# Moving a broadcast and the pool weights in the first loads, and carrying the PSUM turn from one phase to the next

## The chip, the cores and the metric

The kernel runs on the 8 NeuronCores of one Trainium2 chip (two dies, cores 0 to 3 and 4 to 7). Each core does one prompt sequence of 2048 tokens and 16 of the 128 sample tokens; no core waits for another. The metric is the device time of the slowest core in microseconds (us). Engines are called as the profile calls them: PE (matmuls), PEld (weight loads of PE), ACT, DVE, POOL, and SP, which here only issues DMAs. POOL issues DMAs too; those of the weight matrices here also turn f32 into bf16 (W_k, 1024 x 1024 values, lands as 2048 KB).

Some executions were in a slower state: one die then had a granted PE clock of 0.84 to 0.92 instead of 0.99, and the time was 1783 to 1920 us. Only fast executions are compared here.

## The reference, cut to what matters

Two layers. Layer 0 mixes tokens with causal pooling, layer 1 with a short gated convolution; after the mixer each layer has a cross-attention to 256 memory rows and a squared-ReLU MLP.

```
for i in range(2):
    u = rmsnorm(x, g_mix[i])
    if i == 0: y, st = pool_mixer(u, ...)   # window means minus the token, per-group 256x256 map w_pool, times scale
    else:      y, st = conv_mixer(u, ...)   # [B, C, h] = u @ W_in;  y = W_out(B * conv3(C * h))
    x = x + y
    x = x + mem_attend(rmsnorm(x, g_attn[i]), mem_k[i], mem_v[i], w_q[i], w_o[i])
    x = x + sq_relu_mlp(rmsnorm(x, g_ffn[i]), w_up[i], w_down[i])
return rmsnorm(x, g_final), ...             # also the last 15 normalised rows (times g_mix) of the pooling layer
```

## The kernel before: the parts that matter

Every operation is put on an engine's queue by a helper; the helpers find from the addresses who must wait for whom. An engine, and SP with its DMAs, works through its queue in order: a DMA that must wait holds up all later DMAs of its queue. In the kernel before (core 4), SP issued the g_mix broadcast only at 54.91 us, when the spill issued at 46.84 us had landed, and the next x load behind it at 55.39 us.

The **prelude** (about the first 100 us) loads the 16 blocks of x (128 tokens, 512 KB each), normalises them (stA), pools them (stB), transposes them and adds the mapped pooling (stC). Between these steps it prepares the memory rows. x goes through a ring of 7 buffers, so block `tb + 7` is loaded when stC has read block `tb`.

```
# GBC (the broadcast g_mix row) and MEMN1 (memory rows for layer 1) share their bytes
GBC = so.alloc(F32, [D]);  MEMN1 = T(GBC.off, BF16, [NCH, NMEM])
...
xload(0); dma(SP, GV2, gv); xload(1)
dma(POOL, SCB(), <pool_scale row, broadcast to 128 partitions>, "wpf")
dma(POOL, BANDS(), bands)
for cc in range(2):
    dma(POOL, WPF[cc](), wpool_d[:, cc*128:(cc+1)*128, :].rearrange("g p e -> p g e"), "wpf")   # runs of 1 KB
xload(2); <mem rows>; xload(3) .. xload(6)                      # SP
dma(POOL, SK(), W_k);  dma(POOL, SQ_(), W_q)
...
def poolw():                                    # the "scaling": WP = w_pool * g_mix * scale, eight DVE operations
    ...
def stC(tb):
    ...                                         # transposes, WP products, evacuation
    if tb + NXB < 16: xload(tb + NXB)
def mem_turn(k):                                # steps 3 and 4
    ...
    if k == 3:
        spill.append(dma(SP, memn_d, MEMN1))                    # write the memory rows to DRAM
        dma(SP, GBC(), <g_mix row, broadcast to 128 partitions>)  # must wait until the spill has landed
```

In its main loop step s runs stB(s-1), stC(s-2), stA(s+1), then extra work: gains in step 0, poolw in step 1, memory rows in steps 2 to 4, products with W_k from step 9 on.

**PSUM banks** are handed out in turn. Prelude and conv use eight banks, attention and MLP seven, because bank 7 holds the sums of the samples there. A matmul into a bank waits until whoever reads that bank has finished; at the start of layer 1's attention PE waited 3.56 us for such a read by DVE (core 4).

```
def nxt():
    b = bank_ctr[0] % bank_mod[0]; bank_ctr[0] += 1
    return b
def attn_phase(l, fill=()):
    bank_mod[0] = 7
    ...
```

The last conv tile ends with channel chunk 7, whose gate product (DVE) reads a bank at the very end. Right after it layer 1's attention starts: score product m=0, score product m=1, then the output product of that last conv tile (conv_out), which needs all gates.

The softmax here doesn't subtract the row's maximum and nothing guards it: scores larger than these inputs give would overflow.

## Time and profile before

| | before |
|---|---|
| time, median of 3 runs | 1661.63 us (1660.75 to 1663.36) |
| span of the profiled execution, slowest core (core 4) | 1663.1 us |
| PE busy | 1582.0 us, 95% |
| granted clock, mean of each core | 0.989 to 0.991 |

From the page of the kernel before: the span, the busy time of each engine, and the shares of the chain of work that ended last.

```profile
span 1663.1 us, 28460 instructions; the slowest of 8 cores (1656.8 to 1663.1 us)
...
PE 1582.0 (95%) x10064; PEld 902.0 (54%) x10064; DVE 876.0 (53%) x1934; ACT 567.0 (34%) x1074; POOL 114.6 (7%) x245
...
PE 88%; DVE 4%; DMA 2%; ACT 2%; issue 2%; DVEq 0%; POOL 0%; ACTq 0%; SPq 0%; POOLq 0%
```

PE, busy for 95% of the span and 88% of this chain, is the limit nearly everywhere, so the question is where it stands still. The same chain in order of time, in the prelude (start us, length us, what):

```profile
3.55 17.21 DMA MEM<-w_pool
20.86 0.28 DVE MEM L326
...
21.27 5.84 DVE MEM L326 x4
...
46.84 8.00 DMA memn<-MEM
...
54.91 0.33 SPq L353
...
55.39 14.11 DMA MEM<-x
```

First, everything hangs on w_pool's arrival and its scaling on DVE (L326). Then, at 46.84 us, on the spill (memn), on SP's issue of the g_mix broadcast behind it, and on an x load issued at 55.39 us that takes 14.11 us to land. The timeline of PE shows what it does meanwhile (start us, length us, engine, line, operation, count; in brackets the idle time before, and what ended it):

```profile
core 4 of [0, 1, 2, 3, 4, 5, 6, 7], span 1663.1 us
...
62.11 1.89 PE L291 MATMUL PS<-MEM 128*128 128x512 bf16 x8
72.50 4.71 PE L295 MATMUL PS<-MEM 128*128 128x128 bf16 x40 [8.50 <-ACT MEM L342]
77.01 2.44 PE L291 MATMUL PS<-MEM 128*128 128x512 bf16 x8
79.29 2.62 PE L295 MATMUL PS<-MEM 128*128 128x128 bf16 x40
```

PE stands for 8.50 us, and the first 40 matmuls after that take 4.71 us, where the same 40 take 2.62 us later. PE's other standstill of interest is at the start of layer 1's attention, in the timeline of PE:

```profile
core 4 of [0, 1, 2, 3, 4, 5, 6, 7], span 1663.1 us
...
985.93 4.27 PE L291 MATMUL PS<-MEM 128*128 128x400 bf16 x24 [1.01 <-DVE MEM L330]
993.75 6.52 PE L291 MATMUL PS<-MEM 128*128 128x416 bf16 x20 [3.56 <-DVE MEM L330]
```

### The profile page before, as it was taken

To read this page: it belongs to the slowest core of one execution; us is meant where nothing else is said; L and a number is where in the kernel's file an instruction comes from. 1 tells how busy PE (TensorE), PEld (TensorE's weight loads), DVE (VectorE), ACT (ScalarE), POOL (GpSimd) and SP (SyncE) were. 2 spreads that over 40 slices of the span, in tenths; PEclk is the share of its full clock that TensorE was granted. 3 is DMA by queue.
4 is the path that set the end of the run, shared out by engine and by line. 5 is a ranking of instruction groups with operands and counts; after the bars stand their busy time and mean duration, and the time that the engine had idled before them with its cause. 6 is when DMAs were issued, how large, how long until landed. Compare 5 with 4: busy or idle time off the path is not lost.

```text
span 1663.1 us, 28460 instructions; the slowest of 8 cores (1656.8 to 1663.1 us)
## 1 busy us (share of the span) xinstructions
PE 1582.0 (95%) x10064; PEld 902.0 (54%) x10064; DVE 876.0 (53%) x1934; ACT 567.0 (34%) x1074; POOL 114.6 (7%) x245
## 2 busy tenths in 40 slices
PE   3799999999999999999999989999999999999885
PEld 3675555555555555555555545555555655555543
DVE  4465675655444344436566665765564444432356
ACT  4566344541122222231222225444532111123542
POOL 2002110110000000000000001210110000000000
PEclk9899999999999999999999999999999999999998
DMA  9849794575537606246000027894546642000122
GB/s 234 200 78 155 159 168 99 117 147 79 87 67 126 112 1 102 30 76 104 1 1 1 1 44 123 161 174 110 115 90 102 100 61 57 1 1 1 42 80 85
DMA packets 84614, 145.14 MB, mean 87 GB/s; under 512 B 4334, under 2 KB 37358, under 8 KB 84460
## 3 DMA queue, kind: packets, MB, share of 16 engines
q0 software_dynamic: 67568, 84.08, 34.5%
q1 hardware_dynamic: 16908, 59.24, 10.5%
q8 instruction: 84, 1.38, 0.3%
q14 instruction: 54, 0.44, 0.1%
HBM read 212.42 MB, written 14.36 MB: 136 GB/s over the span
## 4 chain that ended last, share of the span: by engine, by line
PE 88%; DVE 4%; DMA 2%; ACT 2%; issue 2%; DVEq 0%; POOL 0%; ACTq 0%; SPq 0%; POOLq 0%
PE PS L291 86%; DVE MEM L326 2%; ACT MEM L318 2%; PE PS L295 2%; DVE MEM L347 1%; DMA MEM<-w_pool 1%; DMA MEM<-x 1%; DMA memn<-MEM 0%; ACT MEM L307 0%; PE PS L300 0%; DVE MEM L344 0%; DVE MEM L330 0%; DVE MEM L338 0%; ACT MEM L342 0%; POOL MEM L353 0%
## 5 line engine op out<-in xcount | busy, mean ns | idle before, releaser
L291 PE MATMUL PS<-MEM 128*128 128x416 bf16 (+5 forms) x8960 | 1503.1, 328 | 16.6 <-DVE MEM L326 7.3
L291 PEld LDWEIGHTS PS<-MEM 128*128 128x128 bf16 (+1 forms) x8960 | 832.3, 98 | 677.6 <-issue 56.0
L318 ACT ACTIVATE MEM<-PS 128x416 f32<-128x416 f32 (+6 forms) x509 | 260.3, 516 | 647.0 <-PE PS L291 626.1
L330 DVE TENSOR_TENSOR MEM<-PS,MEM 128x416 f32<-128x416 f32 (+5 forms) x525 | 294.9, 581 | 253.6 <-PE PS L291 245.3
L330 DVE TENSOR_TENSOR MEM<-MEM 128x416 bf16<-128x416 f32 (+3 forms) x282 | 160.0, 584 | 198.3 <-ACT MEM L318 189.8
L326 DVE SCALAR_TENSOR_TENSOR MEM<-MEM 128x416 bf16<-128x416 f32 (+7 forms) x322 | 181.1, 614 | 128.7 <-ACT MEM L318 107.7
L318 ACT ACTIVATE MEM<-MEM 128x416 bf16<-128x416 f32 (+10 forms) x305 | 186.2, 622 | 180.8 <-DVE MEM L330 113.3
L303 DVE SCALAR_TENSOR_TENSOR MEM<-MEM,PS 128x256 f32<-128x256 f32 x256 | 105.2, 420 | 72.4 <-PE PS L291 48.7
L295 PE MATMUL PS<-MEM 128*128 128x128 bf16 (+4 forms) x896 | 61.7, 248 | 31.2 <-DVE MEM L326 10.4
L342 ACT COPY MEM<-PS 128x512 f32<-128x512 f32 (+3 forms) x73 | 39.1, 536 | 130.3 <-PE PS L291 116.4
L295 PEld LDWEIGHTS PS<-MEM 128*128 128x128 bf16 (+2 forms) x896 | 48.8, 107 | 46.3 <-issue 44.8
L342 ACT CAST MEM<-PS 128x512 bf16<-128x512 f32 (+2 forms) x73 | 39.7, 555 | 66.2 <-PE PS L291 64.8
L344 DVE CAST MEM<-PS 128x512 bf16<-128x512 f32 (+1 forms) x68 | 43.8, 656 | 11.6 <-PE PS L291 11.6
L353 POOL DMA_DIRECT2D MEM<-cv x64 | 47.6, 744 | 13.8 <-PE PS L291 13.8
L318 ACT ACTIVATE PS<-PS 128x416 f32<-128x416 f32 (+3 forms) x67 | 33.1, 494 | 41.3 <-PE PS L291 41.1
L347 DVE TENSOR_REDUCE MEM<-MEM 128x1 f32<-128x1024 f32 (+2 forms) x20 | 24.2, 1209 | 40.8 <-ACT MEM L318 40.8
L300 PE MATMUL PS<-MEM 128*128 128x128 f32 (+6 forms) x208 | 25.1, 268 | 20.6 <-DVE MEM L326 9.8
L350 POOL MEMSET MEM<- 128x4 bf16 (+1 forms) x96 | 15.0, 159 | 358.9 <-PE PS L295 271.6
L326 DVE SCALAR_TENSOR_TENSOR MEM<-PS,MEM 128x512 f32<-128x512 f32 (+2 forms) x40 | 28.1, 743 | 15.5 <-ACT MEM L318 15.5
L300 PEld LDWEIGHTS PS<-MEM 128*128 128x128 f32 (+6 forms) x208 | 21.2, 133 | 24.3 <-issue 23.1
L338 DVE TENSOR_SCALAR MEM<-MEM 128x1024 bf16<-128x1024 f32 (+1 forms) x18 | 13.6, 753 | 36.9 <-ACT MEM L318 36.9
L353 POOL DMA_DIRECT2D MEM<-w_up x36 | 20.6, 582 | 138.0 <-PE PS L291 138.0
(27 smaller groups left out, 131.3 us busy)
## 6 DMA issues: line engine op xcount, KB each, us to landing
MEM<-ck SPq DMA_DIRECT2D x64, 512.0 KB, 5.9
MEM<-cv POOLq DMA_DIRECT2D x64, 256.0 KB, 6.0
MEM<-w_down POOLq DMA_DIRECT2D x6, 2048.0 KB, 17.6
MEM<-x SPq DMA_DIRECT2D x16, 512.0 KB, 15.1
MEM<-w_kv POOLq DMA_DIRECT2D x4, 2048.0 KB, 18.3
MEM<-w_o POOLq DMA_DIRECT2D x4, 2048.0 KB, 23.3
MEM<-w_up POOLq DMA_DIRECT2D x32, 256.0 KB, 12.1
MEM<-w_up POOLq DMA_DIRECT2D x4, 2048.0 KB, 17.1
```

Of the source, the lines that this page charges most:

```text
L291: P.add(PE, "c", lambda e, o=out.ap, l=lhsT.ap, r=rhs.ap: e.matmul(out=o, lhsT=l, rhs=r, start=start, stop=stop), [lhsT, rhs], [out])
L295: P.add(PE, "c", lambda e, o=out.ap, l=lhsT.ap, r=rhs.ap: e.matmul(out=o, lhsT=l, rhs=r, start=start, stop=stop, is_transpose=is_transpose ...
L300: P.add(PE, "c", lambda e, o=out.ap, i=in_.ap, d=ident.ap: e.transpose(out=o, in_=i, identity=d), [in_, ident], [out])
L303: P.add(DVE, "c", lambda e, o=out.ap, a=in0.ap, b=in1.ap, c=acc.ap: e.scalar_tensor_tensor(out=o, in0=a, scalar=1.0, in1=b, op0=ALU.mult, ...
L318: P.add(ACT, "c", lambda e, o=out.ap, i=in_.ap: e.activation(out=o, in_=i, func=func, bias=bias, scale=sc), rd, [out])
L326: P.add(eng, "c", lambda e, o=out.ap, a=in0.ap, b=in1.ap: e.scalar_tensor_tensor(out=o, in0=a, scalar=sc, in1=b, op0=op0, op1=op1), rd, [out])
L330: P.add(eng, "c", lambda e, o=out.ap, a=in0.ap, b=in1.ap: e.tensor_tensor(out=o, in0=a, in1=b, op=op), [in0, in1], [out])
L342: P.add(ACT, "c", lambda e, o=out.ap, i=in_.ap: e.copy(out=o, in_=i), [in_], [out])
L344: P.add(eng, "c", lambda e, o=out.ap, i=in_.ap: e.tensor_copy(out=o, in_=i), [in_], [out])
L347: P.add(eng, "c", lambda e, o=out.ap, i=in_.ap: e.tensor_reduce(out=o, in_=i, axis=AX.X, op=ALU.add), [in_], [out])
L350: P.add(eng, "c", lambda e, o=out.ap: e.memset(o, val), [], [out])
L353: return P.add(q, "d", lambda e, o=out.ap, i=in_.ap: e.dma_start(out=o, in_=i), [in_], [out], chan=chan, after=after)
```

## The change

Its intent: let the loads that the prelude waits for go first, and let the banks continue in turn from conv to attention. By the counter, layer 1's attention used to begin with bank 3, so its second score product took bank 4, which the last gate product had yet to read; now it begins with bank 0.

```diff
-    wpool_d = din("w_pool", [4, 256, 256])
+    wpool_d = din("w_pool", [2, 128, D])          # rearranged on the host: rows of 4 KB
...
+        dma(POOL, BANDS(), DV(bands_d), "wp")
         dma(POOL, SCB(), <pool_scale row, broadcast>, "wpf")
-        dma(POOL, BANDS(), DV(bands_d), "wp")
         for cc in range(2):
-            dma(POOL, WPF[cc](), DV(wpool_d[:, cc * 128:(cc + 1) * 128, :].rearrange("g p e -> p g e")), "wpf")
+            dma(POOL, WPF[cc](), DV(wpool_d[cc].rearrange("p (g e) -> p g e", g=4)), "wpf")
...
-        dma(POOL, SQ_(), <W_q>)                   # was right behind W_k
...                                                # in poolw(), behind POOL's own scaling:
+            dma(POOL, SQ_(), <W_q>)
...                                                # in stC(tb):
-            if tb == 10:
+            if tb == 11:
+                dma(SP, GBC(), <g_mix row, broadcast>, "gbc")
                 dma(SP, XSR(p=(0, NS)), DV(xs_d), "xsr")
...                                                # in mem_turn(3), behind the spill:
-                dma(SP, GBC(), <g_mix row, broadcast>, "gbc")
...                                                # samples_a: result in place (XSR) instead of UF
-            stt(UF(p=P16), XSR(p=P16), st_(2, 18, P16), GBC(p=P16), ALU.mult, ALU.mult)
+            stt(XSR(p=P16), XSR(p=P16), st_(2, 18, P16), GBC(p=P16), ALU.mult, ALU.mult)
...
     def attn_phase(l, fill=()):
+        bank_ctr[0] = bank_ctr[0] % 8 % 7
         bank_mod[0] = 7
```

More of the change, by code (lines that the diff above doesn't have):

```diff
@@ L513, in prelude @@
         dma(POOL, SK(), DV(wsrc_sq(wsrc["wk0"])), f"w{slot_of['wk0']}")
-        dma(POOL, SQ_(), DV(wsrc_sq(wsrc["wq0"])), f"w{slot_of['wq0']}")
         cp(IDB(), IDF())
@@ L528, in poolw @@
                 tt(WPS(cc), WPF[cc](), SCB(), ALU.mult, eng=POOL)
+            dma(POOL, SQ_(), DV(wsrc_sq(wsrc["wq0"])), f"w{slot_of['wq0']}")
             for i in range(2):
@@ L577, in stC @@
                 xload(tb + NXB)
-            if tb == 10:
+            if tb == 11:
+                dma(SP, GBC(), DV(gv_d[R_MIX:R_MIX + 1, :].broadcast_to([128, D])), "gbc")
                 dma(SP, XSR(p=(0, NS)), DV(xs_d), "xsr")
@@ L601, in mem_turn @@
                 spill.append(dma(SP, DV(memn_d), V(MEMN1.ap.rearrange("p c n -> p (c n)"), MEMN1().ivs), "spill"))
-                dma(SP, GBC(), DV(gv_d[R_MIX:R_MIX + 1, :].broadcast_to([128, D])), "gbc")
         st_ctr = [0]
@@ L660, in samples_a @@
             rstd(18, P16)
-            stt(UF(p=P16), XSR(p=P16), st_(2, 18, P16), GBC(p=P16), ALU.mult, ALU.mult)
-            cp(UCB(p=P16), UF(p=P16))
-            dma(SP, DV(nps_d[:, 14, :]), UF(p=P16), "ucf")
+            stt(XSR(p=P16), XSR(p=P16), st_(2, 18, P16), GBC(p=P16), ALU.mult, ALU.mult)
+            cp(UCB(p=P16), XSR(p=P16))
+            dma(SP, DV(nps_d[:, 14, :]), XSR(p=P16), "ucf")
         def samples_b():
@@ L1440 @@
         "gv": gv, "ident": np.eye(128, dtype=np.float32), "bands": _make_bands(),
-        "w_pool": f(w_pool)[0], "w_conv_in": f(w_conv_in)[0], "w_conv_out": f(w_conv_out)[0],
+        "w_pool": f(f(w_pool)[0].reshape(4, 2, 128, 256).transpose(1, 2, 0, 3).reshape(2, 128, D)), "w_conv_in": f(w_conv_in)[0], "w_conv_out": f(w_conv_out)[0],
         "w_q": f(w_q), "w_qT": f(np.swapaxes(np.asarray(w_q), 1, 2)), "w_kv": f(w_kv), "w_o": f(w_o), "w_up": f(w_up), "w_down": f(w_down),
```

## The prediction

> **What bounds the kernel now.** TensorE: the page has PE busy 1582.0 of 1663.1 us (95%) and the last chain is 88% PE. The change can win only where PE stands still. PE's timeline shows such places in the prelude (0 to 100 us) and at 985 to 994 us (start of layer 1's attention).
>
> **Prelude, by the chain of waits (core 4).**
> - 3.55 to 20.86 us: DMA of w_pool; then eight DVE scalings of it (7.4 us); PE goes on at 27.24.
> - 28 to 58 us: steps of about 2.9 us, limited by ACT.
> - 46.84: the spill of the memory rows (8.00 us). The g_mix broadcast overwrites the spilled tile, so SP waits 7.7 us and issues it at 54.91. The x loads 10 to 14 stand behind it: issued from 55.39, the first lands 14.11 us later (the broadcast took 11.8 us). ACT waits 11.63 us for x; PE has other work for a while and loses 8.50 us (64.0 to 72.5). Afterwards the granted clock is 0.63 for 7.5 us: 40 matmuls take 4.71 us against 2.62, eight wide ones 2.44 against 1.65 to 1.9. [...] The stall costs 8.5 + 2.7 = 11 us.
>
> **What the change moves.**
> 1. g_mix behind all x loads. x10 is issued at about 47 us and should land by 55 to 60, even behind the spill and beside W_q; PE needs it at about 61. Gain 11 us (8 to 12). The broadcast has four steps (over 10 us) of light DMA before its use.
> 2. w_pool as 256 runs of 4 KB instead of 1024 of 1 KB, bands first. Bands landed at 11.7 us, w_pool 9.2 later. I estimate landing at 17 to 19. The scaling can't start before the third x block's normalisation (DVE done at 18.66). Gain 2 us (0 to 3.5).
> 3. W_q is issued after the scaling (about 26 us). W_k lands only at 45.8, so W_q keeps about its place; it landed at 65.7 and is first used near 100. No cost.
> 4. The sample row in place: one dependence less, about 0.
> 5. PSUM turn. Layer 0's is unchanged (counter 113 is 1 modulo 7 and 8). Layer 1 starts with bank 0 instead of 3. Before, the second score product (bank 4) waits until the last gate's DVE product at 993.03 has read it: PE idle 3.56 us. After, PE does that score product (1.4 us) and seven eighths of the first conv_out product (1.2 us) before it needs the gate. Gain 2.6; about 0.9 remain.
>
> The rest is bound by PE and only shifts; no instruction of PE, DVE or ACT is added or removed.
>
> **Sum.** 11 + 2 + 2.6 = 15.6 us: 1661.6 to 1646 us, range 1641.5 to 1651, so within 2%. Chances: faster 0.01, same 0.985, slower 0.005.
>
> **Right if** the profile shows: no PE wait of 8 us near 60 to 72, no SP wait for the spill ahead of x loads; PE's clock near 1 from 57 to 80; the scaling starting at 17 to 19.5 us; attention's start earlier by 11 to 15 us; PE's wait for the last gate down from 3.56 to about 1 us.
>
> **What would make it wrong:** DMA may itself be the limit (its share is full until 69 us): beside W_k and W_q, x10 to x12 may still come late, and only half of the 11 us be won; w_pool may crowd out the third x block; the late broadcast may delay the last rows; the gain at the start may vanish in a wait for x.

The trace of the kernel before shows this of the clock (core 4): PE stood from 64.0 to 72.5 us, and the granted clock was 1.00 until 67 us, 0.50 from 68 to 78 us and 1.00 again from 79 us. The DMA share that the prediction calls full was 0.98 to 1.08 in the windows from 62 to 70 us. The landing of w_pool at 17 to 19 us was my estimate from the bands' 11.7 us and the 9.2 us behind them; what rows of 4 KB are worth, no run had shown yet.

## The result, and the profile after

| | before | after |
|---|---|---|
| time, median (4 runs each) | 1661.87 us (1660.75 to 1663.36) | 1647.78 us (1647.09 to 1648.44) |
| ratio of fast runs | | 0.9915 (95% interval 0.9897 to 0.9932) |
| spans of the 8 cores, profiled execution | 1656.8 to 1663.1 | 1642.3 to 1646.8 |

Ratios here are the mean time of one kernel's fast runs over that of the other's of the same rounds, so not quite the ratio of the medians. The kernel is 14.1 us faster, as the medians have it. A second measurement (run e12 below) gave 0.9907.

In the timeline of PE of core 4 (the same core as shown before), the wait of 8.50 us is gone:

```profile
core 4 of [0, 1, 2, 3, 4, 5, 6, 7], span 1645.8 us
...
60.66 1.89 PE L291 MATMUL PS<-MEM 128*128 128x512 bf16 x7
62.47 2.62 PE L295 MATMUL PS<-MEM 128*128 128x128 bf16 x40
64.92 1.89 PE L291 MATMUL PS<-MEM 128*128 128x512 bf16 x7
66.65 2.62 PE L295 MATMUL PS<-MEM 128*128 128x128 bf16 x40
```

The 40 matmuls take 2.62 us each time. SP's timeline of core 4 shows the reason: the five x loads follow the spill at once, and the g_mix row (gv) comes 29 us later.

```profile
45.82 0.33 SPq L353 DMA_DIRECT2D memn<-MEM  x1
46.30 10.40 SPq L353 DMA_DIRECT2D MEM<-x  x5
...
75.37 0.39 SPq L353 DMA_DIRECT2D MEM<-gv  x1
```

The loads did not get quicker by this, they were only issued earlier. The first of the five (x10), issued at 46.30 us, could be used by ACT at 59.55, 13 us later, where before it took 14.11 us. ACT still waits for it, but PE has other work meanwhile. ACT's timeline of core 4:

```profile
59.55 1.06 ACT L307 ACTIVATE MEM<-MEM 128x1024 bf16<-128x1024 f32 x1 [3.04 <-DMA MEM<-x]
```

The start of the prelude, in the chain of the page's core (core 6), has hardly moved:

```profile
3.31 17.65 DMA MEM<-w_pool
21.05 0.28 DVE MEM L326
...
21.45 5.84 DVE MEM L326 x4
```

And at the start of layer 1's attention, in PE's timeline of core 4, the wait of 3.56 us has become one of 0.96 us, with full speed behind it (102 matmuls in 17.66 us, 0.17 us each):

```profile
974.78 6.87 PE L291 MATMUL PS<-MEM 128*128 128x400 bf16 x39 [1.37 <-DVE MEM L330]
982.60 17.66 PE L291 MATMUL PS<-MEM 128*128 128x400 bf16 x102 [0.96 <-DVE MEM L330]
```

**A ruler for all runs.** The cores differ by some us, and the slowest one decides the time. So I read five marks on every core of every profiled execution: A, the start of the scaling on DVE; B, a PE wait of 0.84 us early in layer 0's attention; C, PE's first wait for a gate in the last conv tile; D, a PE wait of about 1 us for ACT in layer 1's attention (1166 us in before's core 4); and the end. B, C and D are read where the wait ends. Means over the eight cores, in us:

| run | A | A to B | B to C | C to D (lowest to highest core) | D to end |
|---|---|---|---|---|---|
| before | 20.87 | 135.02 | 827.94 | 178.98 (177.13 to 180.15) | 497.04 |
| changed | 19.74 | 125.82 | 828.31 | 174.19 (174.16 to 174.23) | 496.78 |
| difference | -1.1 | -9.2 | +0.4 | -4.8 | -0.3 |

The differences sum to -15.0 us of mean span. So the gain has three parts: the scaling 1.1 us earlier, the stretch with the x stall 9.2 us shorter, and the start of layer 1's attention 4.8 us shorter. A to B and C to D need experiments. B to C grew by as much as the wait that ends at C, which went from 1.01 to 1.38 us; why that wait grew was not tested.

### The profile page after: what moved, and what is told of

It is laid out like the page before. It is cut to its first block, busy times and chain, and to the rows that moved or that the text cites. A ratio compares the mean times of both kernels' runs of the same rounds, so it can differ in the third digit from the quotient of the medians.

```text
span 1646.8 us, 28460 instructions; the slowest of 8 cores (1642.3 to 1646.8 us)
## 1 busy us (share of the span) xinstructions
PE 1578.3 (96%) x10064; PEld 900.4 (55%) x10064; DVE 875.3 (53%) x1934; ACT 567.0 (34%) x1074; POOL 114.1 (7%) x245
## 3 DMA queue, kind: packets, MB, share of 16 engines
q1 hardware_dynamic: 16908, 59.24, 10.3%
q8 instruction: 84, 1.38, 0.3%
## 4 chain that ended last, share of the span: by engine, by line
PE 88%; DVE 5%; issue 2%; ACT 2%; DMA 1%; DVEq 0%; POOL 0%; ACTq 0%; SPq 0%; POOLq 0%
PE PS L291 85%; DVE MEM L326 3%; PE PS L295 3%; ACT MEM L318 2%; DVE MEM L347 1%; DMA MEM<-w_pool 1%; DVE MEM L330 0%; DVE MEM L344 0%; PE PS L300 0%; ACT MEM L307 0%; DMA y<-MEM 0%; ACT MEM L342 0%; DVE MEM L338 0%; DVE MEM L303 0%; DVEq L1364 0%
## 5 line engine op out<-in xcount | busy, mean ns | idle before, releaser
L353 POOL DMA_DIRECT2D MEM<-cv x64 | 47.6, 744 | 13.8 <-PE PS L291 13.8
```

Of the source, the lines that this page charges most:

```text
L353: return P.add(q, "d", lambda e, o=out.ap, i=in_.ap: e.dma_start(out=o, in_=i), [in_], [out], chan=chan, after=after)
```

## The experiments

All outputs are right. Each ratio is against the kernel before in the same rounds; the table at the end has the marks.

### One part of the change at a time

**e1_turn_only**: the kernel before with one line added.

```diff
     def attn_phase(l, fill=()):
+        bank_ctr[0] = bank_ctr[0] % 8 % 7
```

> The kernel before, with only the PSUM turn carried from conv to attention. Theory (the second score product waits for the bank of the last gate): PE's wait for the last gate near 990 us falls from 3.56 to about 1 us, everything ahead of it is unchanged, time 2.2 to 2.6 us shorter. Rival (the wait only moves to the next product that needs the gate): the sum of the PE waits there stays near 4.6 us and the time is the same within 1 us.

Measured: ratio 0.9972 (0.9959 to 0.9985), 1658.16 us against 1662.8. This is 4.6 us, more than either theory allowed. PE's waits at the place (core 4) went from 1.01 and 3.56 us to 1.01 and 1.04 us, so 2.5 us of waiting is gone, as the theory says. But C to D shrank by 4.3 us in the mean, to 174.69, and the spread over the cores fell from 3 us to 0.1 us. Something besides the wait has gone. PE's timeline of core 4:

```profile
982.55 6.86 PE L291 MATMUL PS<-MEM 128*128 128x400 bf16 x39 [1.01 <-DVE MEM L330]
990.45 9.80 PE L291 MATMUL PS<-MEM 128*128 128x400 bf16 x57 [1.04 <-DVE MEM L330]
```

**e2_gmix_only**: the kernel before, with the broadcast moved.

```diff
-                dma(SP, GBC(), <g_mix row, broadcast>, "gbc")     # in mem_turn(3)
...
-            if tb == 10:
+            if tb == 11:
+                dma(SP, GBC(), <g_mix row, broadcast>, "gbc")
```

> The kernel before, with only the g_mix broadcast moved behind the x loads. Theory (spill wait and broadcast ahead of x10 cause the stall): PE's idle time of 6 to 8.7 us near 64 to 72 us disappears and the granted clock stays near 1 there; time 9.5 to 11.5 us shorter. Rival (the prelude is limited by DMA bandwidth, and the order hardly matters): x10 to x12 still come late, PE waits 4 us or more between 58 and 75 us, and at most 6 us are gained.

Measured: ratio 0.9946 (0.9933 to 0.9959), which is 9.0 us, slightly below the expected range. A to B is 125.40 us, as in the changed kernel. C to D keeps its spread (176.95 to 179.75). The first theory holds; the rival falls.

**e3_pool_only**: all the rest (rows of 4 KB, bands first, W_q later, row in place).

> Everything else of the change: w_pool as 4 KB rows, bands ahead of the scale row, W_q issued late, the sample row in place; g_mix and the PSUM turn as before. Theory (the 4 KB rows gain about 2.6 us of landing, but the reordered first loads give it back): the scaling starts 0 to 2 us earlier, and the x stall behind the broadcast swallows what is left, so the time is the same within 1 us. Rival (the startup gain counts in full): 2 us shorter.

Measured: ratio 0.9993 (0.9979 to 1.0008), so no gain that the runs resolve. The scaling started 1.5 us earlier in the mean of the profiled cores, and A to B was unchanged (134.96). The expectation's 2.6 us are from the traces: w_pool landed 9.2 us behind the DMA ahead of it in the kernel before (core 4), 6.6 us in the changed kernel (core 6); over the cores it was 6.1 to 9.2 us and 6.3 to 7.0 us. The three parts sum to 0.9911 (1 - 0.0028 - 0.0054 - 0.0007), which agrees with the whole.

**e4_scale_first**: the changed kernel with the scale row again ahead of the bands.

```diff
-        dma(POOL, BANDS(), DV(bands_d), "wp")
         dma(POOL, SCB(), <pool_scale row, broadcast>, "wpf")
+        dma(POOL, BANDS(), DV(bands_d), "wp")
```

> The changed kernel with the scale row's broadcast put ahead of the bands again. Theory (the slow broadcast hides in the slow first microseconds when it goes first, as it did before, where scale row and bands were in by 11.7 us instead of 14.4): w_pool is in 1 to 2.5 us earlier, the scaling starts at 18 to 19.5 us on most cores, the time is 0 to 1.5 us shorter than the changed kernel's (0.9915 of before), so about 0.991. Rival (the order of these two makes no difference): w_pool lands as in the changed kernel, 17.5 to 21 us, and the ratio is 0.9915.

Measured: ratio 0.9906 (0.9891 to 0.9922), the scaling starts at 19.35 us in the mean (18.11 to 21.00) against 19.74 for the changed kernel. That is inconclusive: the cores differ by more. What the expectation calls slow: the scale row took 10.9 us from issue to landing in the changed kernel and 7.7 us before (core 4), and the DMAs of core 4 before moved 70 GB/s from 2 to 4 us, 164 from 4 to 6, and 300 to 344 from 6 to 14.

### What made x late: SP's wait, or the broadcast in the queue?

Moving the broadcast took away two things at once: SP's 7.7 us wait for the spill, and 512 KB ahead of the x loads. Two kernels put one of them back.

**e5_broadcast_no_wait**: the broadcast at its old place, but into memory that the spill doesn't use, so SP does not wait.

```diff
         WPF = [sk.alloc(F32, [4, 256]) for _ in range(2)]
+        GBC = T(WPF[0].off, F32, [D])                             # free after the scaling
...
+                dma(SP, GBC(), <g_mix row, broadcast>, "gbc")     # in mem_turn(3); removed from stC(11)
```

> The changed kernel (0.9915 of before), but the g_mix broadcast issued at its old place, ahead of x10, into memory that the spill does not use, so that SP does not wait for the spill. Theory A (SP's 7.7 us wait for the spill made the x loads late): time as the changed kernel, ratio 0.9905 to 0.992. Theory B (the slow broadcast itself, ahead of the x loads in the same queue, made them late): x10 lands at 60 us or later instead of about 59, PE waits 1 to 4 us between 58 and 70 us, ratio 0.9925 to 0.9945.

**e6_wait_no_broadcast**: the wait at its old place, with one row of 4 KB instead of the broadcast.

```diff
                 spill.append(dma(SP, ...))
+                dma(SP, GBC(p=(0, 1)), DV(gv_d[R_MIX:R_MIX + 1, :]), "gbc0")
```

> The changed kernel, with one row of g_mix (4 KB) loaded onto the spilled tile at the old place, so that SP waits for the spill as before, but without the broadcast of 512 KB. Theory A: the stall is back, PE stands 6 us or more near 64 to 72 us, ratio 0.996 to 0.998. Theory B: x10 is issued near 55 us and lands by 61 us, PE waits 1 us or less, ratio 0.991 to 0.9925.

Measured: e5 0.9934 (0.9922 to 0.9947), e6 0.9951 (0.9937 to 0.9964). Neither theory holds alone: the stall had two causes, and each of them alone brings a part of it back. The wait is the larger one: in the same rounds e6 is 2.7 us slower than e5 (medians 1654.38 and 1651.71 us). Their sizes are less sure, since the changed kernel did not run in these rounds. Against its 0.9915 the broadcast costs 3.2 us and the wait 6.0 us, against its 0.9907 (e12) 4.5 and 7.3 us, and by A to B 4.7 and 5.7 us. My expectation for e6 under theory B, that x10 would land by 61 us, was too hopeful. The timelines of PE, first of e5, then of e6:

```profile
core 4 of [0, 1, 2, 3, 4, 5, 6, 7], span 1649.0 us
...
64.28 4.71 PE L295 MATMUL PS<-MEM 128*128 128x128 bf16 x40 [4.04 <-DVE MEM L338]
```

```profile
core 4 of [0, 1, 2, 3, 4, 5, 6, 7], span 1651.1 us
...
54.05 3.00 SPq L353 DMA_DIRECT2D MEM<-x  x5
...
63.08 1.06 ACT L307 ACTIVATE MEM<-MEM 128x1024 bf16<-128x1024 f32 x1 [7.62 <-DMA MEM<-x]
...
66.00 4.72 PE L295 MATMUL PS<-MEM 128*128 128x128 bf16 x40 [4.49 <-ACT MEM L342]
```

In e6, x10 was issued at 54.05 us on SP's idle queue and ACT could use it at 63.08 us: a load of 512 KB took 9 us beside W_q's load (on core 5, W_q was issued at 24.6 us and landed at 62.1), where the quickest x load of each core of the changed kernel that I looked at (0, 2, 4 and 6) took 4.8 to 6.5 us. That W_q's load made x10's longer fits these landing times, but was not tested alone. In e5 the spill and the broadcast stand ahead of x10 in SP's queue, in the changed kernel the spill alone. Note that I had called the broadcast "slow": over the eight cores it took 9.1 to 11.8 us before, but 4.1 to 4.9 us in the changed kernel, where it is issued at 71.8 to 76.3 us, W_q has landed by 66.1 us on every core, and the next weight load is issued at 88.5 us at the earliest. That the company made it slow fits this, but was not tested alone.

### What the 3.56 us wait really cost

e1 gained 4.6 us from a wait that shrank by 2.5 us. The new theory: behind this wait some cores run at a lower clock, because PE stood idle. The windows of before, 8 us around and behind the wait, for two cores (us, busy us of each engine with counts, granted clock, DMA share, GB/s). Core 4:

```profile
core 4: us, PE busy (x) PEld busy (x) DVE busy (x) ACT busy (x) POOL busy (x), PEclk, DMA share, GB/s
985.00:993.00 8.00, 4.27 (x24) 2.27 (x24) 5.83 (x18) 2.04 (x4) 2.43 (x5) 0.99 0.41 132
993.00:1001.00 8.00, 7.25 (x26) 3.36 (x27) 1.16 (x3) 0.52 (x1) 0.00 (x0) 0.58 1.03 148
```

Core 6:

```profile
core 6: us, PE busy (x) PEld busy (x) DVE busy (x) ACT busy (x) POOL busy (x), PEclk, DMA share, GB/s
985.00:993.00 8.00, 4.44 (x26) 2.37 (x25) 4.41 (x13) 1.55 (x3) 2.44 (x5) 1.00 0.66 100
993.00:1001.00 8.00, 8.00 (x49) 4.60 (x47) 3.28 (x6) 0.00 (x0) 0.00 (x0) 1.00 1.08 151
```

Same wait, but core 4 then did 26 matmuls at a clock of 0.58 where core 6 did 49 at 1.00. In the second window six of the eight cores had 0.58 to 0.84, and exactly these have C to D of 178.9 to 180.2 us; cores 3 and 6, with 1.00, have 177.1. In windows of 1 us the clock of each of these six is 0.50 for 2 to 6 us (core 4: from 993 to 999 us) and then 1.00 again; on cores 3 and 6 it is 1.00 from 986 to 1002 us. So the same wait, 3.55 to 3.56 us on all eight, was followed by half the clock on six cores and by the full clock on two; no run shows why. The kernels that keep the old turn, e2 and e3, show the same: waits of 3.48 to 3.63 us, and in each five of eight cores at 0.59 to 0.81 (windows 982 to 990 us in e2, 990 to 998 us in e3). In the prelude I had counted this cost; here I forgot it.

**e7_fill_wait** tests it: keep the old turn and the wait, but let PE do useless matmuls within it.

```diff
                 if k == 0:
+                    if l == 1 and m == 0:
+                        for _ in range(12):
+                            mm(PSv(OBK, 0, TW), ONESB(), BT[0](0), True, True)   # bank 7, overwritten later
```

> The kernel before, old PSUM turn, with twelve useless matmuls (2.1 us, into the idle bank 7) between the first and the second score product of layer 1, where PE waits 3.56 us for the last gate. Theory (the wait itself cost 2.8 us, and on some cores the idle PE's clock was then halved for some us, 1.7 to 3.1 us more): the wait stays, idle time falls to about 1.4 us, the granted clock is 1.0 in the 8 us after it on all eight cores, the stretch from PE's wait in the last conv tile to its wait at 1166 us takes 177.0 us on all cores (before 177.1 to 180.2), time 1 to 2.5 us shorter. Rival (the extra comes from something later in the attention): that stretch still spreads by 2 to 3 us over the cores and the time is the same within 0.5 us.

Measured: C to D is 177.21 to 177.24 us on all eight cores, and the remaining PE wait at the place is 1.50 to 1.52 us, with a clock of 1.00 in the 8 us windows behind it. The timeline of PE, and below it such a window (columns as above):

```profile
core 4 of [0, 1, 2, 3, 4, 5, 6, 7], span 1655.7 us
...
989.23 5.96 PE L291 MATMUL PS<-MEM 128*128 128x416 bf16 x34 [1.52 <-DVE MEM L330]
...
990.00:998.00 8.00, 8.00 (x49) 4.62 (x48) 2.63 (x5) 0.52 (x1) 0.00 (x0) 1.00 1.07 168
```

Useless work made the stretch 1.8 us shorter in the mean. The rival falls. The time itself, 0.9991 (0.9979 to 1.0003), does not resolve this, since the slowest core's prelude moves by more. So the turn's 4.8 us are 1.8 us of clock (178.98 - 177.22) and 3.0 us (177.22 - 174.19) of the wait itself and what else the turn moves.

### A version that beats both

**e8b_start_wq**: w_pool on SP's queue, ahead of x1; scaling ahead of the second block's normalisation; W_q in step 8.

```diff
         dma(SP, GV2(p=(0, NGV)), DV(gv_d), "c")
+        for cc in range(2):
+            dma(SP, WPF[cc](), DV(wpool_d[cc].rearrange("p (g e) -> p g e", g=4)), "wpq")
         xload(1)
...                                                # the same loads removed from POOL's queue; scale row ahead of bands
         stA(0)
+        gains(); poolw()                          # were in steps 0 and 1
...                                                # in stC(tb)
+            if tb == 6:
+                dma(POOL, SQ_(), <W_q>, after=(P.last[PE],))
```

> An attempt to beat both kernels. The changed kernel, with w_pool loaded from SP right behind the first x block, scale row ahead of bands on POOL's queue, the scaling in program order ahead of the second block's normalisation, and W_q held back until step 8. Theory (attention's start follows the start of the scaling one to one, 125.5 us later): the scaling starts at 11 to 14 us instead of 17.5 to 22, attention starts 4 to 8 us earlier, ratio 0.986 to 0.989. Rival (the prelude's DMA is the limit right behind it): x blocks or W_k come late, PE waits between 25 and 60 us, and 2 us or less are gained (0.990 or more).

Measured: 0.9944 (0.9930 to 0.9957), about 5 us slower than the changed kernel; the rival holds. The scaling did start earlier (16.13 us in the mean), but A to B grew from 125.8 to 134.0 us. PE's timeline:

```profile
core 4 of [0, 1, 2, 3, 4, 5, 6, 7], span 1647.4 us
...
21.91 6.50 PE L295 MATMUL PS<-MEM 128*128 128x128 bf16 x80 [9.74 <-DVE MEM L338]
34.95 0.45 PE L300 MATMUL PS<-MEM 128*128 128x128 f32 x1 [6.54 <-DVE MEM L338]
```

x1, x3 and the memory rows came late: on core 5, ACT waited for x1 until 21.14 us (12.51 in the changed kernel) and for x3 until 33.97 us (no wait there), and the memory rows took 21.8 us to land (median of two; 16.7). Once w_pool had left POOL's queue, W_k (2 MB) was no longer behind it and loaded beside the x blocks: issued at 2.8 us, it landed at 38.1 us on core 5, against 42.6 us in the changed kernel.

**e9_order**: the same, with W_k held back until the scaling is done.

```diff
-        dma(POOL, SK(), <W_k>)
...                                                # in poolw(), after the scaling
+            dma(POOL, SK(), <W_k>, after=(P.last[DVE],))
...                                                # W_q and the spooled state together in stC(6)
```

> The failed attempt (w_pool from SP behind the first x block, scaling first) once more, but W_k is held back until the scaling is done, and W_q with the spooled state until step 8. There, W_k started at 14 us beside w_pool and x1, which came at 17.5 and 21 us, later than without the attempt. Theory (W_k took engine time from the loads that the chain waits for): w_pool lands at 10 to 13 us, x1 by 15 us, the scaling starts at 11 to 14 us, attention starts 2 to 8 us earlier than the changed kernel's 145.6 us, ratio 0.986 to 0.990. Rival (the first 30 us are bound by the bytes themselves): the scaling may start earlier, but x1 to x4 and the memory rows come too late to use it, PE waits 5 us or more for them before 45 us, or W_k comes after 58 us, and the ratio is 0.991 or more.

The 14 us at which this has W_k start is my estimate: on core 5 of e8b the bands, ahead of W_k in POOL's queue, landed at 13.8 us.

Measured: 0.9907 (0.9890 to 0.9923). The scaling starts at 14.28 us, 5.5 us earlier than in the changed kernel, but A to B is 129.35, so B comes only 1.9 us earlier. Between e8b and e9 the release of W_k was the main thing that differed (the spooled state moved too), and A to B fell by 4.7 us: W_k beside the first x blocks was indeed costly. That e9 beats the changed kernel is not resolved by its own run.

**e10_eight_banks**: the changed kernel, where bank 7 joins the turn in layer 1 once the samples are done.

```diff
         def settle():
             mini_b()
+            if l == 1:
+                bank_ctr[0] = bank_ctr[0] % 7
+                bank_mod[0] = 8
```

> The changed kernel, and in layer 1 the eighth PSUM bank joins the turn once the last sample's sums have left it. In the final normalisation four blocks need two banks each, so with seven banks the last block's second half waits for the first block's (PE waits of 2.16, 1.0, 0.3 and 0.3 us in each of four tiles). Theory: one product of 1.5 us fewer stands behind the last block in each tile; time 4 to 6.5 us shorter than the changed kernel's, ratio 0.9875 to 0.989. Rival (the waits only move, since the chain of ACT and DVE per block, 3.3 us, sets the pace): ratio 0.991 to 0.992.

Measured: 0.9892 (0.9877 to 0.9907); D to the end is 493.43 us, against 496.78. The gain is 3.4 us, close to but just below the expected 4 to 6.5. PE's timelines of the changed kernel and of e10, each at its first final tile:

```profile
1527.83 3.22 PE L300 MATMUL PS<-MEM 128*128 128x128 f32 x28
1533.20 0.69 PE L300 MATMUL PS<-MEM 128*32 128x128 f32 x4 [2.15 <-DVE MEM L326]
```

```profile
1527.07 3.66 PE L300 MATMUL PS<-MEM 128*128 128x128 f32 x32
1532.44 2.97 PE L291 MATMUL PS<-MEM 128*128 128x416 bf16 x16 [1.72 <-DVE MEM L326]
```

With eight banks all 32 transposes go through without a wait, and two products can follow at 1532.44. A wait of 1.72 us for DVE stays, so more banks alone do not remove it.

**e11_both**: e9 and e10 together. **e12_changed_again**: the changed kernel in the same rounds.

> The reordered first loads of e9 and the eight banks of e10 together, on top of the changed kernel. If the two are independent (e9 gained 0 to 2 us in the prelude, e10 about 3.7 us in the final normalisation): ratio 0.987 to 0.9895, faster than the changed kernel and than e9. Rival (e9's gain is noise): as e10 alone, 0.989 to 0.990.

> The changed kernel unaltered, on the same chip as e11, so that the two can be compared in the same rounds. Expected ratio 0.9905 to 0.992 as in its first measurement, and 2 to 6 us slower than e11. In its profile the stretch from PE's wait in the last conv tile to its wait near 1149 us should again be 174.2 us on all cores.

Measured: e11 0.9874 (0.9858 to 0.9891), with fast runs of 1642.62 to 1642.99 us (three of four; the fourth was slow); e12 0.9907 (0.9891 to 0.9924), with four fast runs of 1647.15 to 1648.55 us. So e11 is about 5.5 us faster than the changed kernel by the medians of the fast runs of the same rounds (1642.71 and 1648.16 us), and beats both kernels. Its marks say where: D to end -4.0 us against e12, B -1.3 us. The second is within what the cores' starts differ by.

Marks of all runs, means over the cores as above:

| run | A | A to B | C to D (lowest to highest) | D to end | ratio to before |
|---|---|---|---|---|---|
| e1 | 20.57 | 134.48 | 174.69 (174.62 to 174.73) | 496.91 | 0.9972 |
| e2 | 20.48 | 125.40 | 178.12 (176.95 to 179.75) | 497.28 | 0.9946 |
| e3 | 19.36 | 134.96 | 178.19 (176.88 to 179.63) | 497.04 | 0.9993 |
| e4 | 19.35 | 125.52 | 174.22 (174.16 to 174.31) | 497.00 | 0.9906 |
| e5 | 19.12 | 130.56 | 174.30 (174.29 to 174.32) | 496.94 | 0.9934 |
| e6 | 19.16 | 131.56 | 174.22 (174.16 to 174.27) | 497.20 | 0.9951 |
| e7 | 20.29 | 134.38 | 177.22 (177.21 to 177.24) | 497.20 | 0.9991 |
| e8b | 16.13 | 134.04 | 174.38 (174.36 to 174.40) | 497.07 | 0.9944 |
| e9 | 14.28 | 129.35 | 174.38 (174.36 to 174.40) | 497.21 | 0.9907 |
| e10 | 18.99 | 126.01 | 174.19 (174.17 to 174.31) | 493.43 | 0.9892 |
| e11 | 14.47 | 129.34 | 174.38 (174.37 to 174.40) | 492.95 | 0.9874 |
| e12 | 19.50 | 125.61 | 174.18 (174.15 to 174.21) | 496.99 | 0.9907 |

## Why the prediction was right, point by point

The total was right: 1646 us predicted, 1647.78 measured, in the range and within 2%. The places and the waits were right too. But its terms were mis-sized in opposite directions, so that it came so close is partly luck. Two of its own signs were missed by a little: the scaling started at 19.74 us in the mean of the cores, not at 17 to 19.5, and attention started 10.3 us earlier by mark B, not 11 to 15 (11.5 us on core 4, from which the prediction was read).

1. **g_mix behind the x loads, "gain 11 us (8 to 12)".** Right in mechanism, high in size: 9.0 us (e2), 9.2 us by the marks. I took 8.50 us of wait from core 4, the slowest; the mean of the eight cores was 7.24 us. The expected pattern came true: no PE wait there, 40 matmuls in 2.62 us, and a granted clock of 1.00 from 57 to 80 us on all eight cores. e5 and e6 add what the prediction left open: the wait for the spill and the broadcast each cost a part, the wait more. ACT could use x10 at 56.3 to 59.6 us over the cores, within the predicted 55 to 60.
2. **w_pool, "gain 2 us (0 to 3.5)".** 1.1 us by mark A; e3 alone 0.9993, not resolved from nothing. The floor that I named, the third block's normalisation, itself came later: on core 4 DVE finished it at 19.40 us (18.65 + 0.75) instead of 18.66, and w_pool landed at 19.74. The prediction listed this risk ("w_pool may crowd out the third x block"). That w_pool's faster rows caused the delay is argued, not shown.
3. **W_q later, "no cost".** No cost was seen; e3 contains it. On core 4 W_q landed at 66.1 us (24.9 + 41.2), against 65.7 before.
4. **Row in place, "about 0".** Nothing was seen of it; it was not measured alone.
5. **PSUM turn, "gain 2.6; about 0.9 remain".** This is the step that was too small: 4.6 us (e1), 4.8 us by the marks. The wait itself went as predicted, 3.56 to 0.96 us. What was missing is the clock: on six of eight cores it was below full speed after the wait (0.58 to 0.84 from 993 to 1001 us). e7 measures that term at 1.8 us of mean stretch.

So 11 + 2 in the prelude were 9.2 + 1.1, and 2.6 were 4.8. B to C grew by 0.4 us, as the wait at C did; that D to end fell by 0.3 us stays unexplained.

## What to carry to other kernels

When a PE wait is removed, look at the speed of the matmuls behind it too: here C to D became 5.9 us shorter on core 4, whose clock had been at 0.58 behind a wait of 3.56 us, and 3.0 us on core 3, whose clock had stayed at 1.00. With useless matmuls within the wait the clock behind it was 1.00 on all eight cores, and that stretch was 1.8 us shorter, though the time of the whole kernel did not show it. Keep a DMA that must wait, and big loads that nobody needs yet, off the queue of the loads that the next step needs; and when one load is moved to another queue, check what moves up in its place (W_k did, and cost e8b about 5 us). Read a stall on all cores before costing it: the slowest core shows more than the mean.

## What the traces show of the clock and of DMA

- In e5 and e6 all 14 PE gaps of 2.72 to 4.77 us in the prelude were followed by 40 matmuls in 3.62 to 4.72 us, five of these gaps at 2.72 to 3.20 us. The two gaps of 1.80 and 1.83 us were followed by 40 matmuls in 2.62 us. On the other hand, a gap of 3.55 to 3.56 us left the clock at 1.00 on two of eight cores in the kernel before. No one length of gap parts these cases.
- In the fast runs all eight cores had a mean granted clock of 0.987 to 0.996, with PE busy for 95% (before) and 96% (changed) of the profiled executions. Only the slow runs had lower clocks, on one die each (0.84 to 0.92); no run shows what brings that state about.
- One x load issued on an idle queue took 9 us beside another queue's weight load (e6), and the g_mix broadcast 9.1 to 11.8 us beside such a load and 4.1 to 4.9 us late in the changed prelude. How much longer a DMA takes because of another queue's, no run measured alone.
